# The context taps of a 31-wide depthwise convolution: three of eight channel tiles on GpSimd, as a product and a sum

## The chip, the cores and the metric

The kernel runs on one core of a Trainium2 chip. Its engines are TensorE (PE in the profile; PEld is its weight load), VectorE (DVE), ScalarE (ACT), GpSimd (POOL) and SyncE (SP), which issues all transfers here. Each engine runs its own queue in order and waits on semaphores that others raise. The metric is the device time of one execution in microseconds (us); the median of the runs is given, and lower is better.

## The reference

Two layers work on two streams of 256 tokens of 1024 channels: the context and the latent tokens. Each layer has a mixer (one input projection, a gated linear recurrence A and a convolution module B beside it, their gated sum) and a channel part (a SwiGLU in layer 0, eight experts of which each token takes two in layer 1). The second layer needs of the context only the state of the recurrence, so branch B of the context is computed in layer 0 alone. The part that the change touches:

```python
def _dwconv_seq(u, w, b, pad_l, pad_r):        # context: along the 256 tokens
    y = lax.conv_general_dilated(u, w[:, None, :], window_strides=(1,), padding=((pad_l, pad_r),),
                                 feature_group_count=u.shape[-1], ...)
    return y + b

# in _mixer, branch B
v = u_glu * jax.nn.sigmoid(g_glu)
v = _dwconv_rows(v, conv_w, conv_b) if on_grid else _dwconv_seq(v, conv_w, conv_b, CONV_PAD, CONV_PAD)
y_b = jax.nn.silu(_layernorm(v, ln_g, ln_b)) @ w_b
```

CONV_W is 31 and CONV_PAD 15. A channel of the context is thus convolved with its own 31 weights along the tokens; the latent stream is convolved along the columns of a 4 x 64 grid, so that only 7 of the 31 weights meet a token.

## The kernel before

All tiles hold 128 channels (partitions) by up to 512 columns: 256 context tokens and 256 latent ones. Eight such tiles, j = 0 to 7, make the 1024 channels.

**Matmuls.** Weights arrive as raw chunks of four pieces of 128 x 1024 float32 (`chunk`, `hold`; two raw buffers, transfers on SyncE). Each piece is split (`split`, `hilo`) into a rounded part wh on ScalarE (L156) and a remainder wl on VectorE (L157), four buffers of each, and `mm` multiplies each eighth of it three times with the activations (L283 to L285): wh with the high part nh, wh with the low part nl, wl with nh. One piece is 24 matmuls of 512 columns. A raw buffer is free for the next transfer when its four pieces are split. Between the weight chunks stand chunks of the modulation weights, with matmuls of their own (pmod, L394).

**The mixer of layer 0.** After the first projections, the loop over j makes for each tile two pieces of matmuls, pglu and pglg; then ScalarE takes tanh of pglg into v, VectorE makes v = (v + 1) * pglu (L690), and `conv_b` makes cv from v. Between them the recurrence of branch A runs (gates, scans; L555 to L592). The next loop (eight pieces) makes `gel` on ScalarE, multiplies it on VectorE by the recurrence's result (L704), and splits the product into yah on ScalarE (L156) and yal on VectorE (L157). Then follow 16 pieces for the merging gates (gab), and behind these the LayerNorm over cv (`ln_steps`), whose first step is a sum over all cv on TensorE (pcol, L294), with the branch projection beside it.

**The convolution.** `conv_b` makes cv first as the middle tap plus bias over all columns (L599), then the 30 other context taps, each one VectorE instruction over 241 to 255 columns, cv = v shifted * weight + cv (L606), then six latent taps of 64 to 192 columns (L610). All write the same cv, so that each tap waits for the one before.

**What sets the order.** The kernel is recorded in the order of its text, and a scheduler puts each engine's instructions in a fixed order by priorities and estimated times. The splits have a raised priority; `conv_b` is recorded in `later(1000)`, so its taps come 1000 places later in priority than they stand and fill the gaps between other work of VectorE. On the chip each engine keeps the fixed order, whatever happens.

**Buffers.** Tiles of the tag ya share 16 buffers: first the recurrence's results hs and the eight v, then yah and yal, later others. A yah that takes over the buffer of a v waits until the last tap of that v is done. cv has eight buffers of its own.

Of the kernel before, what the change touches and what calls it, by code (L numbers as in the profile page):

```python
# [6 lines left out]
F32 = mybir.dt.float32  # L7
# [3 lines left out]
ALU = mybir.AluOpType  # L11
AX = mybir.AxisListType

P = 128
# [3 lines left out]
TC = 256  # L18
# [21 lines left out]
WHEN0 = {4: (0, 1, -1), 5: (2,), 6: (3, -1), 7: (4,), 8: (5, -1), 9: (6,), 10: (7, -1)}  # L40
WHEN1 = {4: (-1,), 5: (2,), 6: (3,), 8: (-1,), 9: (4,), 10: (5,), 12: (-1,), 13: (6,), 14: (7,), 15: (-1,)}
LAG1 = (0, 0)
SCW = 38
RINGA, RINGB, XB = 9, 5, 1

# [88 lines left out]
class Trunk:  # L134
# [460 lines left out]
    def conv_b(self, i, j, v, cv):  # L595
        nc = self.nc
        w = lambda t: self.v(("vw", i), j * CONVW + t)
        c0 = TC if i == DEPTH - 1 else 0
        nc.vector.tensor_scalar(cv[:, c0:T], v[:, c0:T], w(15), self.v(("vb", i), j), op0=ALU.mult, op1=ALU.add)  # L599
        if c0 == 0:  # L600
            for t in range(CONVW):
                d = t - 15
                if d == 0:
                    continue
                a0, a1 = max(0, -d), TC - max(0, d)
                nc.vector.scalar_tensor_tensor(cv[:, a0:a1], v[:, a0 + d:a1 + d], w(t), cv[:, a0:a1],  # L606
                                               op0=ALU.mult, op1=ALU.add)
        for d in (-3, -2, -1, 1, 2, 3):
            a0, a1 = TC + max(0, -d) * GRID, T - max(0, d) * GRID
            nc.vector.scalar_tensor_tensor(cv[:, a0:a1], v[:, a0 + d * GRID:a1 + d * GRID], w(15 + d),  # L610
                                           cv[:, a0:a1], op0=ALU.mult, op1=ALU.add)
# [235 lines left out]
    def run(self, ctx):  # L847
# [5 lines left out]
        self.mod = [self.cst.tile([P, 48, 2], F32, tag=f"mod{i}", name=f"mod{i}") for i in range(DEPTH)]  # L853
        self.sc = self.cst.tile([P, KD, SCW], F32, tag="sc", name="sc")
        nc.gpsimd.memset(self.mod[1], 0.0)
        nc.sync.dma_start(self.sc, self.vec_d[:, NV:NV + KD * SCW].rearrange("p (k m) -> p k m", m=SCW))
        nc.sync.dma_start(xs, self.xt_d[1])
# [43 lines left out]
        def norm1(s):  # L901
            if s == 0:
                hx1.extend(self.pairs("hx"))
            self.bgs.append(self.norm_steps(1, X, s * TC, (s + 1) * TC, self.gains(1, "n1", 1), 0, hx1, LAG1[s]))

# [495 lines left out]
def layout(inputs):  # L1401
# [5 lines left out]
    xt = np.concatenate([a["ctx"][0], a["x"][0]], axis=0).T.reshape(KD, P, 2, TC).transpose(2, 1, 0, 3)  # L1407
    vec = np.zeros((P, NV + KD * SCW), f32)

    def put(key, m):  # L1410
        vec[:, VO[key]:VO[key] + m.shape[1]] = m
# [14 lines left out]
    put("fg", col(a["final_g"]))  # L1426
    cc = np.zeros((P, KD, SCW), f32)
    cc[:, :, 6] = col(a["c"][0])
# [77 lines left out]
```

## Time and profile before

| | us |
|---|---|
| median of 3 runs (1849.68 to 1850.18) | 1849.96 |
| the profiled execution | 1851.57 |
| its span, first to last instruction | 1849.5 |
| TensorE busy in it | 1805.6 |
| VectorE busy | 1220.4 |
| ScalarE busy | 815.0 |
| GpSimd busy | 0.8 |
| 240 context taps (L606) on VectorE | 102.3 |

The span is what the hardware profiler saw of one execution on the core; the execution's own time holds 2.1 us more around it. An engine's busy time is the sum of its instructions; where they overlap in the engine's pipeline, they are counted once. TensorE's granted clock is 0.991 of full speed over the whole span, and 1.00 in the stretch from 50 us on in which the mixer of layer 0 lies. That mixer spans some 60 to 460 us; the context taps lie between 119 and 301 us.

### The profile page before, as it was taken

The page shows a single profiled execution, that of the slowest core. Times are in us where ns is not written, and L with a number is a line of the kernel's source. Part 1 is how long each engine was busy: PE and PEld are TensorE (multiplying, and loading weights), DVE is VectorE, ACT ScalarE, POOL GpSimd, SP SyncE. Part 2 cuts the span into 40 slices and gives each one's busy share as a digit, 9 for nine tenths or more (in the row PEclk, how much of TensorE's full clock was granted, in tenths as well). Part 3 has the DMA queues.
Part 4 walks back from the last instruction along what each step waited for, and adds up shares of the span by engine and source line. Part 5 has one row for each costly group of instructions (what it writes and reads, how often), then busy time and mean ns, then how long its engine had stood idle before and what let it go on. Part 6 is the DMA issues. An engine that isn't in the chain of part 4 may idle for free.

```text
span 1849.5 us, 26754 instructions
## 1 busy us (share of the span) xinstructions
PE 1805.6 (98%) x10394; PEld 1380.3 (75%) x10394; DVE 1220.4 (66%) x2232; ACT 815.0 (44%) x1177; POOL 0.8 (0%) x6
## 2 busy tenths in 40 slices
PE   8999999999999999999999999999999999999996
PEld 4667777768998888889778899657865776686553
DVE  4899996255679977756899656318933972595112
ACT  3695332253552222224789564216722761474001
POOL 0000000000000000000000000000000000000000
PEclk8999999999999999999999999899999999999998
DMA  9233444231235645521233547699999999999995
GB/s 369 94 141 117 181 182 182 91 110 73 97 120 200 222 178 194 197 91 47 103 119 132 183 180 298 262 419 420 420 387 421 420 392 400 420 420 377 418 419 228
DMA packets 65654, 449.64 MB, mean 243 GB/s; under 512 B 7280, under 2 KB 7408, under 8 KB 23024
## 3 DMA queue, kind: packets, MB, share of 16 engines
q1 hardware_dynamic: 65520, 447.85, 61.6%
q8 instruction: 84, 1.38, 0.3%
q14 instruction: 50, 0.41, 0.1%
HBM read 446.78 MB, written 1.05 MB: 242 GB/s over the span
## 4 chain that ended last, share of the span: by engine, by line
PE 80%; DVE 11%; DMA 5%; ACT 2%; issue 1%; SPq 0%; ACTq 0%; DVEq 0%
PE ps L283 11%; PE ps L285 11%; PE ps L284 11%; PE s L1243 8%; DMA mraw<-in_wm_dram 4%; PE y L1298 4%; PE s L1233 3%; PE s L1232 3%; PE s L1231 3%; DVE wl L157 2%; PE y L1292 2%; PE y L1291 2%; PE y L1290 2%; PE ps L782 2%; PE ps L781 2%; PE ps L783 2%
## 5 line engine op out<-in xcount | busy, mean ns | idle before, releaser
L156 ACT ACTIVATE wh<-raw 128x1024 fp32r<-128x1024 f32 (+1 forms) x237 | 246.7, 1053 | 454.4 <-PE ps L284 287.7
L157 DVE TENSOR_TENSOR wl<-raw,wh 128x1024 fp32r<-128x1024 f32 (+1 forms) x237 | 286.4, 1216 | 132.0 <-ACT wh L156 129.1
L283 PE MATMUL ps<-nh,wh 128*128 128x512 f32 (+1 forms) x736 | 273.2, 371 | 0.7 <-ACT wh L156 0.7
L285 PE MATMUL ps<-nh,wl 128*128 128x512 f32 (+1 forms) x736 | 269.6, 367 | 3.1 <-DVE wl L157 3.1
L284 PE MATMUL ps<-nl,wh 128*128 128x512 f32 (+1 forms) x736 | 269.5, 366 | 0.0
L157 DVE TENSOR_TENSOR wl<-mraw,wh 128x1024 fp32r<-128x1024 f32 x198 | 234.0, 1222 | 24.9 <-ACT wh L156 23.8
L156 ACT ACTIVATE wh<-mraw 128x1024 fp32r<-128x1024 f32 x198 | 202.8, 1055 | 30.1 <-PE s L1232 23.6
L1243 PE MATMUL s<-mraw,xes 128*64 128x256 f32 x1760 | 205.3, 384 | 3.6 <-DMA mraw<-in_wm_dram 3.5
L1243 PEld LDWEIGHTS s<-mraw,xes 128*64 128x64 f32 x1760 | 124.6, 138 | 62.4 <-DMA mraw<-in_wm_dram 4.3
L283 PEld LDWEIGHTS ps<-nh,wh 128*128 128x128 f32 x736 | 139.1, 189 | 31.0 <-issue 2.2
L259 ACT ACTIVATE hd<-s 128x128 f32<-128x128 f32 (+1 forms) x88 | 27.9, 317 | 304.4 <-PE s L1243 279.8
L285 PEld LDWEIGHTS ps<-nh,wl 128*128 128x128 f32 x736 | 139.0, 189 | 27.9 <-DVE wl L157 3.3
L284 PEld LDWEIGHTS ps<-nl,wh 128*128 128x128 f32 x736 | 139.1, 189 | 25.5 <-issue 1.4
L1252 DVE TENSOR_TENSOR hd<-hd,s 128x128 f32<-128x128 f32 (+1 forms) x88 | 29.6, 336 | 174.1 <-ACT hd L259 174.1
L1233 PE MATMUL s<-wl,xe 128*128 128x512 f32 x264 | 104.9, 397 | 4.2 <-DVE wl L157 4.2
L1298 PE MATMUL y<-mraw,hs 128*64 128x512 f32 x440 | 104.5, 595 | 3.2 <-DMA mraw<-in_wm_dram 1.7
L1231 PE MATMUL s<-wh,xe 128*128 128x512 f32 x264 | 106.6, 404 | 0.0
L1232 PE MATMUL s<-wh,xe 128*128 128x512 f32 x264 | 103.7, 393 | 0.0
L606 DVE SCALAR_TENSOR_TENSOR cv<-v,vec,cv 128x251 f32<-128x251 f32 (+14 forms) x240 | 102.3, 469 | 0.7
L235 DVE SCALAR_TENSOR_TENSOR junk<-wv,scr 128x512 f32<-128x512 f32 x128 | 84.1, 686 | 0.2
L283 PE MATMUL pglu<-nh,wh 128*128 128x256 f32 (+1 forms) x192 | 64.6, 337 | 1.0 <-ACT wh L156 1.0
L1233 PEld LDWEIGHTS s<-wl,xe 128*128 128x128 f32 x264 | 49.5, 188 | 19.6 <-DVE wl L157 8.9
(290 smaller groups left out, 3433.8 us busy)
## 6 DMA issues: line engine op xcount, KB each, us to landing
mraw<-in_wm_dram SPq DMA_DIRECT2D x264, 1024.0 KB, 11.6
raw<-in_wd_dram SPq DMA_DIRECT2D x64, 2048.0 KB, 8.0
wv<-in_wv_dram SPq DMA_DIRECT2D x96, 256.0 KB, 3.8
lw<-in_wd_dram SPq DMA_DIRECT2D x16, 256.0 KB, 2.8
raw<-in_wd_dram SPq DMA_DIRECT2D x2, 1024.0 KB, 14.9
xs<-in_xt_dram SPq DMA_DIRECT2D x1, 1024.0 KB, 4.9
xc<-in_xt_dram SPq DMA_DIRECT2D x1, 1024.0 KB, 7.9
scr<-in_sr_dram SPq DMA_DIRECT2D x4, 256.0 KB, 8.7
```

The costliest lines, as they stand in the source:

```text
L156: return (self.nc.scalar.activation(hi, src, AF.Copy), self.nc.vector.tensor_tensor(lo, src, hi.bitcast(F32), op=ALU.subtract))
L157: self.nc.vector.tensor_tensor(lo, src, hi.bitcast(F32), op=ALU.subtract))
L235: nc.vector.scalar_tensor_tensor(junk, w[h], 1.0, rows[2 * s + h], op0=ALU.mult, op1=ALU.mult, accum_out=acc[:, h, s:s + 1])
L283: self.nc.tensor.matmul(o, wh, ah, start=(k == 0), stop=False)
L284: self.nc.tensor.matmul(o, wh, al, start=False, stop=False)
L285: self.nc.tensor.matmul(o, wl, ah, start=False, stop=(k == KD - 1))
L606: nc.vector.scalar_tensor_tensor(cv[:, a0:a1], v[:, a0 + d:a1 + d], w(t), cv[:, a0:a1], op0=ALU.mult, op1=ALU.add)
L1231: nc.tensor.matmul(p1, xe[0][:, k, :], wh[:, cs], start=(k == 0), stop=False)
L1232: nc.tensor.matmul(p1, xe[1][:, k, :], wh[:, cs], start=False, stop=False)
L1233: nc.tensor.matmul(p1, xe[0][:, k, :], wl[:, cs], start=False, stop=(k == KD - 1))
L1243: nc.tensor.matmul(p1[r, 0:2 * P].rearrange("p (g f) -> p g f", g=2), xe[:, k, :], w[:, :, h * P:(h + 1) * P], start=(k == 0), stop=(k == ...
L1298: ins = self.nc.tensor.matmul(py[0][r, :], hs[:, f * HALF:(f + 1) * HALF], raw[:, f * PIECE + q * 512:f * PIECE + (q + 1) * 512], start=(c ...
```

## The change

For the channel tiles j = 1, 3 and 5 the 30 context taps leave VectorE. Each becomes two GpSimd instructions: a product of the shifted v and the weight into a new tile tap (two buffers, in the pool of the recurrence's weights), and a sum of cv and tap into cv. The middle tap with the bias and the six latent taps of these tiles stay on VectorE. Taps of the other five tiles are as they were. In the changed program lines stand 1 (behind line 42) to 6 (behind line 606) further down: L606 is L612, L610 is L616, L156 is L157, L259 is L260.

```diff
+POOLED = (1, 3, 5)
...
                 a0, a1 = max(0, -d), TC - max(0, d)
+                if j in POOLED:
+                    p = self.lrup.tile([P, TC], F32, tag="tap", name="tap")
+                    nc.gpsimd.tensor_scalar(p[:, a0:a1], v[:, a0 + d:a1 + d], w(t), None, op0=ALU.mult)
+                    nc.gpsimd.tensor_tensor(cv[:, a0:a1], cv[:, a0:a1], p[:, a0:a1], op=ALU.add)
+                    continue
                 nc.vector.scalar_tensor_tensor(cv[:, a0:a1], v[:, a0 + d:a1 + d], w(t), cv[:, a0:a1],
                                                op0=ALU.mult, op1=ALU.add)
```

The order of TensorE and of the transfers stays. On GpSimd, behind the two memsets at the kernel's start, stood before nothing but the test at the end of the kernel (names are tiles with their buffer numbers; in brackets the semaphores that an instruction waits for):

```order
L1501 UNCONDITIONAL_BRANCH [waits barrier_Pool_Activation_PE_DVE_SP_gather]
L855 MEMSET mod1_64 128x96
L876 MEMSET wz_95 128x512
L1381 TENSOR_LOAD cint_10514 [waits DVE_49]
L1154 COMPARE_AND_BRANCH
```

Now 180 instructions and one more ahead of them stand there; tile j = 1 has v_1062 and cv_1065:

```order
L882 MEMSET wz_95 128x512
L609 ISA
L609 TENSOR_SCALAR tap_1067<-v_1062,vec_58 128x241 [waits DMAHW0_49,DVE_49]
L609 TENSOR_SCALAR tap_1070<-v_1062,vec_58 128x242
L610 TENSOR_TENSOR cv_1065<-cv_1065,tap_1067 128x241 [waits DVE_49,PE_49,Pool_49]
L610 TENSOR_TENSOR cv_1065<-cv_1065,tap_1070 128x242 [waits Pool_49]
L609 TENSOR_SCALAR tap_1073<-v_1062,vec_58 128x243
L609 TENSOR_SCALAR tap_1076<-v_1062,vec_58 128x244 [waits Pool_49]
L610 TENSOR_TENSOR cv_1065<-cv_1065,tap_1073 128x243 [waits Pool_49]
```

They come in groups of two products and two sums; three of four wait for an earlier one of GpSimd's own, and the first of a tile for VectorE.

On ScalarE, where the stage of gel begins (yah is the rounded part of gel's product, wh that of the weight pieces), the order before was:

```order
L259 ACTIVATE gel_1890<-ps_1865 128x512 [waits PE_49]
L156 ACTIVATE yah_1893<-gel_1890 128x512 [waits DVE_49]
L156 ACTIVATE wh_1982<-raw_1980 128x1024 [waits DMAHW0_49,Activation_49]
L156 ACTIVATE wh_2018<-raw_1980 128x1024 [waits Activation_49]
L156 ACTIVATE wh_2054<-raw_1980 128x1024 [waits PE_49,Activation_49]
L259 ACTIVATE gel_1926<-ps_1901 128x512 [waits PE_49]
L156 ACTIVATE yah_1929<-gel_1926 128x512 [waits DVE_49]
L156 ACTIVATE wh_2090<-raw_1980 128x1024 [waits PE_49,Activation_49]
L259 ACTIVATE gel_1973<-ps_1937 128x512 [waits PE_49]
L156 ACTIVATE yah_1976<-gel_1973 128x512 [waits DVE_49]
```

The same place now:

```order
L260 ACTIVATE gel_2070<-ps_2045 128x512 [waits PE_49]
L157 ACTIVATE yah_2073<-gel_2070 128x512 [waits DVE_49,Pool_49]
L157 ACTIVATE wh_2162<-raw_2160 128x1024 [waits DMAHW0_49,Activation_49]
L157 ACTIVATE wh_2198<-raw_2160 128x1024 [waits Activation_49]
L157 ACTIVATE wh_2234<-raw_2160 128x1024 [waits PE_49,Activation_49]
L260 ACTIVATE gel_2106<-ps_2081 128x512 [waits PE_49]
L157 ACTIVATE yah_2109<-gel_2106 128x512 [waits DVE_49,Pool_49]
L157 ACTIVATE wh_2270<-raw_2160 128x1024 [waits PE_49,Activation_49]
L260 ACTIVATE gel_2153<-ps_2117 128x512 [waits PE_49]
L157 ACTIVATE yah_2156<-gel_2153 128x512 [waits DVE_49,Pool_49]
```

The instructions are the same in the same places; the three yah, of j = 1, 2 and 3, wait for GpSimd as well.

On VectorE, just behind the v of tile j = 1 (cv_893 is the cv of tile 0, uc and gi are branch A's), the order before was:

```order
L599 TENSOR_SCALAR cv_1065<-v_1062,vec_58 128x512
L555 SCALAR_TENSOR_TENSOR gi_1110<-gi_1110,uc_709 128x512
L606 SCALAR_TENSOR_TENSOR cv_893<-v_890,vec_58,cv_893 128x250
L555 SCALAR_TENSOR_TENSOR gi_1119<-gi_1119,uc_709 128x512
L606 SCALAR_TENSOR_TENSOR cv_893<-v_890,vec_58,cv_893 128x249
L606 SCALAR_TENSOR_TENSOR cv_1065<-v_1062,vec_58,cv_1065 128x241
L606 SCALAR_TENSOR_TENSOR cv_893<-v_890,vec_58,cv_893 128x248
L157 TENSOR_TENSOR wl_1400<-raw_1397,wh_1399 128x1024
L606 SCALAR_TENSOR_TENSOR cv_893<-v_890,vec_58,cv_893 128x247
L606 SCALAR_TENSOR_TENSOR cv_1065<-v_1062,vec_58,cv_1065 128x242
```

And now:

```order
L600 TENSOR_SCALAR cv_1065<-v_1062,vec_58 128x512
L556 SCALAR_TENSOR_TENSOR gi_1170<-gi_1170,uc_709 128x512
L612 SCALAR_TENSOR_TENSOR cv_893<-v_890,vec_58,cv_893 128x250
L556 SCALAR_TENSOR_TENSOR gi_1179<-gi_1179,uc_709 128x512
L612 SCALAR_TENSOR_TENSOR cv_893<-v_890,vec_58,cv_893 128x249
L616 SCALAR_TENSOR_TENSOR cv_1065<-v_1062,vec_58,cv_1065 128x64
L612 SCALAR_TENSOR_TENSOR cv_893<-v_890,vec_58,cv_893 128x248
L158 TENSOR_TENSOR wl_1520<-raw_1517,wh_1519 128x1024
L612 SCALAR_TENSOR_TENSOR cv_893<-v_890,vec_58,cv_893 128x247
L616 SCALAR_TENSOR_TENSOR cv_1065<-v_1062,vec_58,cv_1065 128x128
```

In the places of the context taps of tile 1 stand its latent taps, which came later before.

## Rows read from the trace of the kernel before

**Rows 1.** The page, section 1: engine, busy us (share of the span), instructions.

```profile
span 1849.5 us, 26754 instructions
...
PE 1805.6 (98%) x10394; PEld 1380.3 (75%) x10394; DVE 1220.4 (66%) x2232; ACT 815.0 (44%) x1177; POOL 0.8 (0%) x6
```

**Rows 2.** Busy time by stretches of 25 us, columns in the first line.

```profile
core 0: us, PE busy (x) PEld busy (x) DVE busy (x) ACT busy (x) POOL busy (x), PEclk, DMA share, GB/s
100.00:125.00 25.00, 25.00 (x101) 18.72 (x100) 24.96 (x42) 23.62 (x33) 0.00 (x0) 1.00 0.29 106
...
175.00:200.00 25.00, 23.45 (x108) 17.34 (x107) 24.74 (x56) 5.62 (x7) 0.00 (x0) 1.00 0.69 253
200.00:225.00 25.00, 25.00 (x120) 19.13 (x119) 25.00 (x58) 7.68 (x10) 0.00 (x0) 1.00 0.44 168
...
275.00:300.00 25.00, 25.00 (x116) 18.77 (x116) 24.54 (x58) 7.31 (x10) 0.00 (x0) 1.00 0.43 169
```

**Rows 3.** Timeline of TensorE: start us, us, instruction, [idle before <- its releaser].

```profile
184.94 0.50 PE L283 MATMUL pglu<-nh,wh 128*128 128x512 f32 x1 [1.02 <-ACT wh L156]
...
186.20 0.50 PE L285 MATMUL pglu<-nh,wl 128*128 128x512 f32 x1 [0.53 <-DVE wl L157]
```

**Rows 4.** The chain of waits there, in order of time: start us, us, what.

```profile
173.72 1.13 DVE wl L157
174.87 8.94 DMA raw<-in_wd_dram
183.83 1.07 ACT wh L156
184.92 1.24 DVE wl L157
```

**Rows 5.** VectorE's last group of taps (timeline); the first use of cv (chain).

```profile
293.28 7.67 DVE L606 SCALAR_TENSOR_TENSOR cv<-v,vec,cv 128x255 f32<-128x255 f32 x15
...
359.99 1.85 PE pcol L294 x16
```

**Rows 6.** Timeline of VectorE: eight taps in a row.

```profile
203.55 3.17 DVE L606 SCALAR_TENSOR_TENSOR cv<-v,vec,cv 128x244 f32<-128x244 f32 x8
```

**Rows 7.** Busy time in four longer stretches, columns as in rows 2.

```profile
146.00:240.00 94.00, 92.45 (x419) 69.82 (x418) 93.74 (x198) 39.52 (x53) 0.00 (x0) 1.00 0.36 132
146.00:174.90 28.90, 28.90 (x121) 22.48 (x120) 28.90 (x57) 19.94 (x28) 0.00 (x0) 1.00 0.07 23
...
254.70:301.00 46.30, 46.30 (x215) 34.61 (x214) 45.75 (x103) 12.82 (x18) 0.00 (x0) 1.00 0.46 182
301.00:360.00 59.00, 59.00 (x270) 46.40 (x272) 15.50 (x15) 16.36 (x22) 0.00 (x0) 1.00 0.32 120
```

**Rows 8.** Timeline of GpSimd: its two larger instructions.

```profile
0.74 0.18 POOL L855 MEMSET mod<- 128x96 f32 x1 [0.29 <-POOLq L1495]
0.85 0.53 POOL L876 MEMSET wz<- 128x512 f32 x1
```

**Rows 9.** Timeline of ScalarE around yah of j = 1, 2, 3.

```profile
227.49 0.63 ACT L156 ACTIVATE yah<-gel 128x512 fp32r<-128x512 f32 x1 [4.44 <-DVE gel L704]
228.02 2.94 ACT L156 ACTIVATE wh<-raw 128x1024 fp32r<-128x1024 f32 x3
...
234.90 0.63 ACT L156 ACTIVATE yah<-gel 128x512 fp32r<-128x512 f32 x1 [3.46 <-DVE gel L704]
235.44 1.04 ACT L156 ACTIVATE wh<-raw 128x1024 fp32r<-128x1024 f32 x1
...
239.74 0.63 ACT L156 ACTIVATE yah<-gel 128x512 fp32r<-128x512 f32 x1 [2.77 <-DVE gel L704]
...
251.91 2.94 ACT L156 ACTIVATE wh<-raw 128x1024 fp32r<-128x1024 f32 x3
```

**Rows 10.** Timeline of VectorE: v of tiles 1, 3 and 5.

```profile
145.00 0.68 DVE L690 SCALAR_TENSOR_TENSOR v<-v,pglu 128x512 f32<-128x512 f32 x1
...
175.42 0.66 DVE L690 SCALAR_TENSOR_TENSOR v<-v,pglu 128x512 f32<-128x512 f32 x1
...
191.40 0.68 DVE L690 SCALAR_TENSOR_TENSOR v<-v,pglu 128x512 f32<-128x512 f32 x1
```

**Rows 11.** Timelines: VectorE's three splits behind these wh, and TensorE's first use.

```profile
254.74 3.49 DVE L157 TENSOR_TENSOR wl<-raw,wh 128x1024 fp32r<-128x1024 f32 x3
...
259.80 0.50 PE L283 MATMUL ps<-nh,wh 128*128 128x512 f32 x1
```

## The prediction before the run

> **What bounds the kernel now.** I read the shares of the engines first [rows 1]: TensorE is busy for 1805.6 of 1849.5 us, VectorE for 1220.4, GpSimd for 0.8. Such a share is a mean over stages, so the table of 25 us windows comes next, over the stretch in which the context taps run [rows 2]. There both engines are full: from 100 to 300 us VectorE is busy for 24.5 to 25 of every 25 us, and TensorE for 25.00 in all but one window. The timeline of TensorE shows its only two idle spells in the stretch, 1.02 and 0.53 us, at 184.94 and 186.20 us [rows 3]. The chain of waits says where they come from [rows 4]: VectorE ends a split (wl) late at 174.8, that frees a raw buffer, the next weight transfer starts at 174.87 and takes 8.94 us, then come wh, wl and the matmul. So VectorE is full, but TensorE waits for it by only 1.55 us. The rest of its work is filler: the taps, which are recorded 1000 places later than their turn and fill the gaps between the splits. The splits come in time, and the last tap, in the group that begins at 293.28, is long over when the convolution's result is summed, at 359.99 [rows 5]. Nothing waits for taps but buffers. **A VectorE with less to do can give back at most these 1.55 us** (0.08%), and a measurement of this kernel can tell about 0.2%, or 3.7 us, from no change.
>
> **What it removes.** 90 taps (three tiles of 30) of VectorE. Eight of them in a row take 3.17 us, one after the other at some 0.39 us [rows 6], so 90 × 0.39 = 35 us of VectorE. The changed order shows where these go. Between the v of tile 1 and the split that frees the raw buffer at 174.8 stand 58 instructions; by the rows' steps they make 28.7 us, against 57 in 28.90 us before [rows 7]: other taps moved up into the holes. The same holds down to the three splits at 254.74, ahead of which the changed order has its last tap. So until about 254 VectorE is as full as it was, the 35 us and some waiting fall off the end (254.7 to 301), where nothing waits for them, and even the 1.55 us stay. What the removal gives: 0.
>
> **What it adds: GpSimd's own time.** 90 products and 90 sums of 241 to 255 columns, in order, each tile's 60 starting when its v and its first term are there. No row shows such an instruction. The nearest are two memsets [rows 8]: 0.18 us for 96 columns and 0.53 us for 512, that is 0.84 ns a column and 0.10 us besides, 0.31 us for one pass over 248 columns. A product reads one tile and writes one: one pass (0.31) to two (0.52). A sum reads two: two passes (0.52) to three (0.73), and one pass (0.31) as the lowest end of all. A pair then costs 0.62 to 1.25 us; I take the middle of the ranges, (0.31 + 0.52)/2 for the product and (0.52 + 0.73)/2 for the sum, some 1.04 us, since one of the pair reads two tiles and the rows are of an instruction that reads none. In most places each waits for the one before, by the order's waits, which pushes towards the upper end. The extra first instruction that the order shows ahead of the taps (ISA) waits for nothing, so it lies 100 us before tile 1's v and costs nothing, unless it takes longer than that.
>
> **What it adds: three waits on ScalarE.** Tiles v of the taps and yah of the next stage share a ring of 16. In the changed order yah of j=1, 2 and 3 wait for GpSimd, in the built program for counts that mean: last product of tile 1, of tile 3, of tile 5. Before, these yah ran at 227.49, 234.90 and 239.74 us [rows 9]. Tile 1's v starts at 145.00, tile 3's at 175.42, tile 5's at 191.40 [rows 10], so from about 146.5 GpSimd has 81 us for 30 pairs, 88 for 60, 93 for 90. Queued behind each yah on ScalarE stand the wh of the coming weight pieces: three behind the first, one behind the second, three more (at 251.91) some way behind the third. TensorE waits for those. The cover for the third: its three splits begin on VectorE at 254.74, the first ends 1.2 us later, and TensorE takes it up at 259.80 [rows 11]; on ScalarE alone there would be some 6 us. I take 5. So **TensorE loses (the end of tile 5's products − 239.7 − 5) us**, if positive. Running alone, GpSimd would be late from (239.7 + 5 − 146.5)/90 = 1.09 us a pair.
>
> **What GpSimd does to VectorE.** This decides the sum, and no row has the two engines at work together: GpSimd is idle in all windows [rows 2]. The lower bound is no effect at all. The upper is that one of them stands still while the other works, turn by turn. Then each of the 180 GpSimd instructions waits for one VectorE instruction and the reverse. VectorE's cost is 93.74 us for 198 instructions from 146 to 240, or 0.47 each [rows 7]; GpSimd's mean is 1.04/2 = 0.52 by the middle above. But part of each is issue and wait, in which the other can go on; with the share that occupies memory at one to two passes for a product and one to two for a sum, 0.31 to 0.52, I take 0.42. The end is then at 146.5 + 180 × (0.47 + 0.42) = 307, and VectorE by then has run 180 of the 198 instructions that it had run by 240, so the splits are as late as GpSimd is: both sides agree. TensorE loses 307 − 239.7 − 5 = 62 us. It is not given back: behind 301 TensorE is again busy for 59.00 of 59.00 us [rows 7]. With 0.31 it is 146.5 + 140 = 287, a loss of 42; with 0.63 (half of 1.25), 345, a loss of 100. I take the turns rather than no effect because both engines work here on nothing but SBUF tiles, the taps, splits and sums each with two inputs.
>
> The Trainium skill states this outright. Its page "SBUF — State Buffer", section "Who interferes with whom", says that VectorE's second read port is GpSimd's only one, so that a VectorE instruction with two SBUF inputs and a GpSimd instruction that reads SBUF exclude one another: whichever starts first holds the port to its end and the other is blocked, not slowed. No run here shows it so far. By that rule the time is the one worked out for the turns, and the rival without effect falls away.
>
> **The sum.** The profiled execution took 1851.57 us (span 1849.5 and 2.1 around it), 1.6 us above the median of the runs, 1849.96. The loss is added to either: 1851.57 + 62 = 1914 for this execution, and **1849.96 + 62 = 1912 us** for the median.
>
> **Rivals.**
> 1. *Side by side, and in time.* GpSimd and VectorE don't hinder one another and a pair takes under 1.09 us; yah waits for nothing new. For it: the bounds from the memsets, 0.62 to 1.25, have their middle just below. Against it: the waits from one instruction to the next come on top. TensorE is full either way, so this ends on the other side of the forecast, not slower: 1848.4 (with the 1.55 us) to 1850. Chance 0.13.
> 2. *Side by side, but late.* No hindrance, a pair above 1.09 us. At 1.25 the end is at 146.5 + 112.5 = 259, 14 us beyond the cover: 1864. With 0.1 us (the fixed part of a memset) for each of three waits in two pairs, 1.4 a pair, 272.5 and 1878. Tile 3's last product would be at 230.5, still in time. Chance 0.20.
> 3. *VectorE always first.* GpSimd gets in only where VectorE pauses. Then yah of j=1 stands at 227.5, VectorE runs out of work behind it, and GpSimd does 90 pairs of 0.83 to 1.04 us from there, with some 15 us of VectorE between the three: 317 to 336, a loss of 72 to 91. This is the forecast's mechanism with another order; I count it there.
> 4. *Faster.* The split at 173.64 comes earlier, the transfer behind it too, and TensorE's 1.55 us vanish. It decides if a tile's taps really left that stretch; the order says no, and even so it is 1848.4, within 0.2%. For more than 3.7 us there is no idle TensorE to fill. Chance of faster by over 0.2%: 0.02.
>
> **How the numbers follow.** Turns (with 3): 0.65, at 1912, by its ends 1892 to 1950. Late alone: 0.20, 1853 to 1880. In time: 0.13. Faster: 0.02. The likeliest is the turns, so 1912. The range leaves out rivals 1 and 4 (0.15) and the top of the turns' ends, about 0.05: 1853 to 1945. Faster 0.02, same 0.13, slower 0.85.
>
> **What would show it.** In the profile of the changed kernel: VectorE's step from tap to tap from 146 us on (0.39 now; near 0.8 to 0.9 if they take turns, 0.39 if not); the spacing of the GpSimd instructions, two of them 1.8 us if turns, near 1.0 if not; ScalarE's yah <- gel waiting for GpSimd at j=2 and j=3; TensorE idle in the windows from 175 on, in sum some 60 us, for wl at first and for wh behind yah later; and the distance from 301 to the end unchanged. It is wrong if VectorE's taps keep their step beside a busy GpSimd, or if a pair takes so long by itself that the waits alone make the loss.

## The result, and the profile after

The changed kernel takes **1929.68 us** (median, 1929.44 to 1930.88), against 1849.96 for the kernel before (the median of three runs; a fourth took 2231.29 us and is not counted), some 80 us more. The measured ratio is **1.0435, with a 95% interval of 1.0423 to 1.0448**; the two medians by themselves give 1.0431. The profiled execution took 1930.88 us, its span 1929.0. The forecast was 1912, by a loss of 62.

Page of the changed kernel, busy time by engine, then the groups of the taps (busy us, mean ns | idle before); to be read against [rows 1]:

```profile
PE 1813.5 (94%) x10394; PEld 1386.0 (72%) x10394; DVE 1227.1 (64%) x2142; ACT 814.4 (42%) x1177; POOL 176.6 (9%) x186
...
L609 POOL TENSOR_SCALAR tap<-v,vec 128x241 f32<-128x241 f32 (+14 forms) x90 | 104.5, 1171 | 143.6 <-DVE v L696 143.6
L612 DVE SCALAR_TENSOR_TENSOR cv<-v,vec,cv 128x241 f32<-128x241 f32 (+13 forms) x150 | 90.0, 624 | 0.6
L610 POOL TENSOR_TENSOR cv<-cv,tap 128x241 f32<-128x241 f32 (+14 forms) x90 | 73.5, 817 | 3.5
```

VectorE has 90 instructions fewer and is busy for 6.7 us *more*. Its remaining taps take 624 ns each in the mean, 469 before. A pair on GpSimd takes 1171 + 817 ns, 1.99 us. TensorE was not busy for 1929.0 - 1813.5 = 115.5 us, against 1849.5 - 1805.6 = 43.9: 71.6 of the span's 79.5 us more are idleness. The other 7.9 are a longer busy time for the same 10394 matmuls.

The windows of the changed kernel (columns as in [rows 2]) say where:

```profile
150.00:175.00 25.00, 25.00 (x109) 20.29 (x108) 25.00 (x38) 13.23 (x18) 24.53 (x24) 1.00 0.00 1
175.00:200.00 25.00, 10.38 (x45) 6.33 (x43) 25.00 (x36) 6.57 (x8) 24.53 (x24) 0.79 0.39 137
200.00:225.00 25.00, 23.29 (x91) 18.80 (x92) 25.00 (x39) 3.67 (x4) 24.53 (x25) 0.87 0.31 116
225.00:250.00 25.00, 19.52 (x89) 14.27 (x88) 25.00 (x40) 4.01 (x5) 24.53 (x25) 0.86 0.44 161
250.00:275.00 25.00, 17.58 (x78) 12.47 (x77) 25.00 (x39) 7.13 (x10) 24.61 (x24) 0.86 0.25 92
275.00:300.00 25.00, 18.90 (x90) 13.90 (x88) 5.99 (x10) 0.00 (x0) 24.45 (x29) 0.98 0.44 160
300.00:325.00 25.00, 0.00 (x0) 0.00 (x0) 1.94 (x4) 1.11 (x2) 23.67 (x30) 0.50 0.02 9
```

There are two parts. From 150 to 275 VectorE is full, yet gets through 36 to 40 instructions in 25 us (49 to 58 before), and TensorE misses 29 us of 125. From 275 on ScalarE stands still, and from 281 on VectorE too, beside a GpSimd that works without a pause. The first loss of TensorE, in its timeline (in brackets the wait before a row and what ended it):

```profile
175.73 0.40 PE L285 MATMUL pglg<-nl,wh 128*128 128x512 f32 x1
186.71 0.79 PE L286 MATMUL pglg<-nh,wl 128*128 128x512 f32 x1 [10.58 <-DVE wl L158]
187.30 0.63 PE L284 MATMUL pglg<-nh,wh 128*128 128x512 f32 x1
```

It waits for a split: the matmul needs the wl that stands in the chain of before at 173.72 [rows 4] and begins now at 185.23 (VectorE's timeline):

```profile
185.23 1.42 DVE L158 TENSOR_TENSOR wl<-raw,wh 128x1024 fp32r<-128x1024 f32 x1
```

From 146.00 to 186.40 VectorE ran 56 instructions in 40.40 us; before, 57 took 28.90 [rows 7]. The second loss begins on ScalarE (its timeline):

```profile
262.29 0.63 ACT L157 ACTIVATE yah<-gel 128x512 fp32r<-128x512 f32 x1 [7.01 <-DVE gel L710]
...
272.24 0.63 ACT L157 ACTIVATE yah<-gel 128x512 fp32r<-128x512 f32 x1 [6.00 <-DVE gel L710]
...
322.40 0.63 ACT L157 ACTIVATE yah<-gel 128x512 fp32r<-128x512 f32 x1 [48.09 <-POOL tap L609]
...
334.55 2.93 ACT L157 ACTIVATE wh<-raw 128x1024 fp32r<-128x1024 f32 x3
```

The yah of j = 3 waits 48.09 us for the last product of tile 5; the wh behind it, at 251.91 before [rows 9], come at 334.55, and TensorE waits 41.75 us for them:

```profile
335.64 0.79 PE L284 MATMUL ps<-nh,wh 128*128 128x512 f32 x1 [41.75 <-ACT wh L157]
```

In that stretch GpSimd shows its own price (two instructions a row):

```profile
288.03 1.81 POOL L609 TENSOR_SCALAR tap<-v,vec 128x249 f32<-128x249 f32 x2
289.81 1.51 POOL L610 TENSOR_TENSOR cv<-cv,tap 128x249 f32<-128x249 f32 x2
```

A product is 0.90, a sum 0.75, a pair 1.65 us with VectorE at rest.

What hinders VectorE is seen by kind of instruction. From 150 to 240 us, the kernel before, then the changed one (split, v made from SBUF and PSUM, middle tap, a context tap, the smallest latent tap):

```profile
L157 DVE TENSOR_TENSOR wl<-raw,wh 128x1024 fp32r<-128x1024 f32 x16 | 19.0, 1218 | 0.3 <-ACT wh L156 0.3
L690 DVE SCALAR_TENSOR_TENSOR v<-v,pglu 128x512 f32<-128x512 f32 x6 | 4.1, 677 | 0.0
L606 DVE SCALAR_TENSOR_TENSOR cv<-v,vec,cv 128x250 f32<-128x250 f32 x7 | 3.3, 475 | 0.0
L610 DVE SCALAR_TENSOR_TENSOR cv<-v,vec,cv 128x64 f32<-128x64 f32 x7 | 2.0, 279 | 0.0
L599 DVE TENSOR_SCALAR cv<-v,vec 128x512 f32<-128x512 f32 x3 | 1.6, 540 | 0.0
```

```profile
L158 DVE TENSOR_TENSOR wl<-raw,wh 128x1024 fp32r<-128x1024 f32 x11 | 14.2, 1315 | 0.0
L600 DVE TENSOR_SCALAR cv<-v,vec 128x512 f32<-128x512 f32 x5 | 3.5, 708 | 0.0
L616 DVE SCALAR_TENSOR_TENSOR cv<-v,vec,cv 128x64 f32<-128x64 f32 x7 | 3.5, 500 | 0.0
L696 DVE SCALAR_TENSOR_TENSOR v<-v,pglu 128x512 f32<-128x512 f32 x5 | 3.4, 671 | 0.0
L612 DVE SCALAR_TENSOR_TENSOR cv<-v,vec,cv 128x250 f32<-128x250 f32 x4 | 2.4, 612 | 0.0
```

Only v <- v, pglu keeps its time (677 and 671): its second input lies in PSUM. The other four grow by 0.10 to 0.22 us each, the smallest the most, so not in proportion to their size: this points to a wait rather than a slower pace. The shortest, median and longest context tap from 146 to 260 us (ns, before, then after) say so too:

```profile
L606 DVE SCALAR_TENSOR_TENSOR cv<-v,vec,cv x148: 458/472/481, 145.6 to 259.3; 128x251 f32<-128x251 f32 x10, 128x250 f32<-128x250 f32 x10, 128x249 f32<-128x249 f32 x10, 128x241 f32<-128x241 f32 x10
```

```profile
L612 DVE SCALAR_TENSOR_TENSOR cv<-v,vec,cv x92: 456/676/951, 146.4 to 259.7; 128x250 f32<-128x250 f32 x7, 128x249 f32<-128x249 f32 x7, 128x248 f32<-128x248 f32 x6, 128x247 f32<-128x247 f32 x6
```

The shortest are as short as ever, the longest have about half a microsecond on top.

### The profile page after: what moved, and what is told of

It is laid out like the page before. It is cut to its first block, busy times and chain, and to the rows that moved or that the text cites. A ratio compares the mean times of both kernels' runs of the same rounds, so it can differ in the third digit from the quotient of the medians.

```text
span 1929.0 us, 26855 instructions
## 1 busy us (share of the span) xinstructions
PE 1813.5 (94%) x10394; PEld 1386.0 (72%) x10394; DVE 1227.1 (64%) x2142; ACT 814.4 (42%) x1177; POOL 176.6 (9%) x186
## 4 chain that ended last, share of the span: by engine, by line
PE 79%; POOL 9%; DVE 7%; DMA 2%; ACT 1%; issue 1%; SPq 0%; DVEq 0%; ACTq 0%
PE ps L284 10%; PE ps L286 10%; PE ps L285 10%; PE s L1249 9%; POOL tap L609 5%; PE y L1304 4%; POOL cv L610 4%; PE s L1239 3%; PE s L1238 3%; PE s L1237 3%; DMA mraw<-in_wm_dram 2%; DVE wl L158 2%; PE y L1298 2%; PE y L1297 2%; PE y L1296 2%; PE ps L788 2%
## 5 line engine op out<-in xcount | busy, mean ns | idle before, releaser
L157 ACT ACTIVATE wh<-raw 128x1024 fp32r<-128x1024 f32 (+1 forms) x237 | 246.7, 1053 | 460.3 <-PE ps L285 289.4
L157 ACT ACTIVATE wh<-mraw 128x1024 fp32r<-128x1024 f32 x198 | 202.8, 1055 | 30.1 <-PE s L1238 24.2
L260 ACT ACTIVATE hd<-s 128x128 f32<-128x128 f32 (+1 forms) x88 | 27.9, 317 | 303.5 <-PE s L1249 278.9
L609 POOL TENSOR_SCALAR tap<-v,vec 128x241 f32<-128x241 f32 (+14 forms) x90 | 104.5, 1171 | 143.6 <-DVE v L696 143.6
L612 DVE SCALAR_TENSOR_TENSOR cv<-v,vec,cv 128x241 f32<-128x241 f32 (+13 forms) x150 | 90.0, 624 | 0.6
L610 POOL TENSOR_TENSOR cv<-cv,tap 128x241 f32<-128x241 f32 (+14 forms) x90 | 73.5, 817 | 3.5
```

What stands on the lines that cost most here:

```text
L157: return (self.nc.scalar.activation(hi, src, AF.Copy), self.nc.vector.tensor_tensor(lo, src, hi.bitcast(F32), op=ALU.subtract))
L609: nc.gpsimd.tensor_scalar(p[:, a0:a1], v[:, a0 + d:a1 + d], w(t), None, op0=ALU.mult)
L610: nc.gpsimd.tensor_tensor(cv[:, a0:a1], cv[:, a0:a1], p[:, a0:a1], op=ALU.add)
```

## The experiments

**Theory:** the loss is of two parts, splits that come late while the engines hinder one another on a full VectorE, and the third yah, which waits for a GpSimd that is slow by itself. **Rivals:** the wait alone; the hindering alone; removal that gains and hides a larger loss. Differences are medians of the comparison, each kernel against the one before on the same chip (1849.1 to 1850.4).

**1. The removal alone.** In conv_b the three lines of the GpSimd taps go:

```diff
                 if j in POOLED:
-                    p = self.lrup.tile([P, TC], F32, tag="tap", name="tap")
-                    nc.gpsimd.tensor_scalar(p[:, a0:a1], v[:, a0 + d:a1 + d], w(t), None, op0=ALU.mult)
-                    nc.gpsimd.tensor_tensor(cv[:, a0:a1], cv[:, a0:a1], p[:, a0:a1], op=ALU.add)
                     continue
```

> The 30 context taps of tiles 1, 3 and 5 are left out on both engines (their sums are missing from the result); all else is as in the changed kernel. It measures the removal alone. My theory: the removal gives nothing but at most the 1.55 us in which TensorE stood idle, so 1848.4 to 1850. Rival: VectorE was a bound after all, the 35 us fewer on it let splits and transfers come earlier, and the time falls below 1846; then what GpSimd costs is larger than the 80 us measured.

Measured: 1850.17 us, ratio 1.0001 [0.9991, 1.0010]. VectorE is busy for 1185.8 us instead of 1220.4: thirty-five microseconds less on it are worth nothing, and the 80 us are the whole price of GpSimd's part.

**2. No yah waits for GpSimd.**

```diff
-        tags = {"ya": 16, "g": 16, "cv": 8, "hx": 16, "lt": 2}
+        tags = {"ya": 16, "pv": 3, "g": 16, "cv": 8, "hx": 16, "lt": 2}
...
-            v = self.t2("ya", "v")
+            v = self.t2("pv" if not last and j in POOLED else "ya", "v")
```

> The changed kernel, but the v of tiles 1, 3 and 5 get three buffers of their own, so that no yah waits for GpSimd; the 180 GpSimd instructions and their company with VectorE stay. My theory has two parts, splits that come late while the two engines hinder one another (TensorE idle some 30 to 35 us from 175 to 275 in the changed kernel) and the third yah, which waits 48 us for GpSimd and makes TensorE wait 41.7 us for wh. Without the second the time is 1880 to 1895, and TensorE's single spell of 40 us is gone. Rival 1, the wait of yah is everything and lateness before it is made up for: 1850 to 1855. Rival 2, hindering is everything and the wait only shows it: 1920 to 1930.

Measured: 1893.13 us, 1.0235 [1.0218, 1.0252], 42.8 us over before. The spell of 41.75 us is gone (TensorE's longest wait of any kind in this stretch is 7.2, for a wl), the late splits stay. Its windows:

```profile
175.00:200.00 25.00, 13.28 (x54) 8.68 (x53) 25.00 (x34) 4.38 (x5) 24.61 (x23) 0.83 0.47 167
200.00:225.00 25.00, 25.00 (x105) 19.30 (x108) 25.00 (x43) 4.92 (x6) 24.53 (x26) 0.90 0.23 86
```

Both rivals fall: it is neither 1850 nor 1930.

**3. Tile 1 alone.** `POOLED = (1,)`.

> Only tile 1's taps go to GpSimd (30 pairs); tiles 3 and 5 have theirs on VectorE, as before. GpSimd is then done near 202 us, ahead of the one yah that waits for it (227), so only hindering is left, from 145 to 202. My theory: TensorE loses what it lost there in the changed kernel, about 15 us in 175 to 200 and a little behind it, and gets none back: 1864 to 1870. Rival, only the waits of yah cost: 1850.

Measured: 1868.12 us, 1.0103 [1.0086, 1.0120], 17.8 us for 30 pairs. TensorE is busy for 13.22 us between 175 and 200 and for 22.54 between 200 and 225, full before and behind. No yah waits for GpSimd there: late splits alone.

**4. The yah's wait with a free VectorE.**

```diff
                     continue
-                nc.vector.scalar_tensor_tensor(cv[:, a0:a1], v[:, a0 + d:a1 + d], w(t), cv[:, a0:a1],
-                                               op0=ALU.mult, op1=ALU.add)
+                continue
```

> The changed kernel with the context taps of the other five tiles left out on VectorE (the result lacks them), so that VectorE has idle time from 146 on and GpSimd has its own pace more of the time. The third wait stands here on the yah of j=2, near 235 us. If GpSimd's own price (1.65 us a pair with VectorE idle) is the larger part of the loss: a pair at 1.65 to 1.9 us, tile 5's products done at 295 to 317, TensorE loses 55 to 77, time 1905 to 1927, nearly all of it in one spell, and none between 175 and 200. If the full VectorE is what makes GpSimd late: a pair near 1.1, done by 246, time below 1860.

Measured: 1909.34 us, 1.0324 [1.0307, 1.0341], 59.0 us. A window by engine, ScalarE's row, then one row of VectorE and two of TensorE:

```profile
175.00:200.00 25.00, 25.00 (x117) 18.93 (x116) 20.02 (x33) 7.08 (x9) 24.48 (x26) 1.00 0.54 213
```

```profile
310.73 0.63 ACT L157 ACTIVATE yah<-gel 128x512 fp32r<-128x512 f32 x1 [78.42 <-POOL tap L609]
```

```profile
260.34 1.17 DVE L158 TENSOR_TENSOR yal<-gel,yah 128x512 fp32r<-128x512 f32 x1 [31.15 <-POOL tap L609]
```

```profile
263.20 0.80 PE L286 MATMUL ps<-nh,wl 128*128 128x512 f32 x1 [13.04 <-DVE wl L158]
...
316.83 0.80 PE L284 MATMUL ps<-nh,wh 128*128 128x512 f32 x1 [43.62 <-ACT wh L157]
```

Nothing is lost from 175 to 200. TensorE loses in two spells, not in one as expected. With the taps gone, the ring of buffers turns differently: a yal on VectorE waits until 260.34 for the last product of tile 3, the wl behind it comes late, and TensorE waits 13.04 us. The yah of j = 2 waits until 310.73 for the last product of tile 5, and TensorE waits 43.62 us. Both are waits for a buffer that GpSimd still reads. A pair takes 1120 + 808 ns = 1.93 us: with most of VectorE's company gone, GpSimd is late by its own price.

**5. Both at once.** The edits of 2 and 4 together.

> Both at once: own buffers for the v of tiles 1, 3 and 5, so that no yah waits for GpSimd, and no context taps of the other five tiles on VectorE, so that it has idle time (the result lacks those taps). All 180 GpSimd instructions stay. If the loss is made of these two alone, late splits on a full VectorE and the wait of yah: GpSimd still needs 150 to 170 us and stretches what runs beside it, but TensorE loses nothing or next to it, 1848 to 1853. If a stretched split costs TensorE something even when VectorE has idle time: 1858 to 1880.

Measured: 1849.22 us, 0.9999 [0.9989, 1.0009], with all 180 instructions on GpSimd, at 1237 + 864 ns a pair, until some 329 us. Its splits are stretched all the same, and TensorE loses nothing (splits from 150 to 280 us, then one window):

```profile
L158 DVE TENSOR_TENSOR wl<-raw,wh 128x1024 fp32r<-128x1024 f32 x22 | 28.5, 1325 | 21.0 <-ACT wh L157 21.0
```

```profile
175.00:200.00 25.00, 25.00 (x116) 18.93 (x116) 19.66 (x31) 6.04 (x8) 24.53 (x26) 1.00 0.59 236
```

So the four corners are 1929.7 (VectorE full, yah waits), 1893.1 (full, no wait), 1909.3 (free, wait), 1849.2 (free, no wait). The parts, 43 and 59, come to more than 80 together. A TensorE that is already late meets the waiting yah later: it runs out of work for it at 293.89 in the changed kernel and at 273.21 in run 4 (335.64 - 41.75 and 316.83 - 43.62).

**6. Another place.** Tile 7 alone, its own v buffer, its GpSimd taps recorded behind the last gel with one small product of yah ahead of them:

```diff
+POOLED = (7,)
...
             ya.append((hi, lo))
+            if j == 7 and not last:
+                self.conv_b(i, 7, v, cv[7], hi)
```

> Only tile 7's 30 taps go to GpSimd, with a v buffer of its own, and behind the last yah (289 us before), where VectorE's taps are nearly over and VectorE has idle time between its splits. A pair at 1.66 us: done near 340, ahead of the sum over cv at 360. If hindering costs only where VectorE is full or where somebody waits for GpSimd: 1848 to 1852, though splits there are stretched. If each GpSimd instruction beside a split costs TensorE time wherever it lies, at the rate of the run with tile 1 alone (18 us for 30 pairs): 1860 to 1868.

Measured: 1849.01 us, 1.0000 [0.9990, 1.0010]. That yah came at 272.96 instead of 288.96, with 30 taps fewer on VectorE, so GpSimd worked from 274 on, beside a VectorE that was busy for 17.79 us from 275 to 300 (24.54 before). TensorE is busy for 25.00 us of every 25 from 200 to 375. Thirty pairs cost 18 us in one place and nothing in the other.

**7. Does writing hinder?** Memsets in place of products and sums; in the second version they stand behind tile 1's v:

```diff
+                    if t == 0:
+                        nc.gpsimd.tensor_tensor(self.wide[:, 15:TC], cv[:, 15:TC], v[:, 0:TC - 15], op=ALU.add)
+                        continue
+                    nc.gpsimd.memset(self.wide, 0.0)
+                    nc.gpsimd.memset(self.wide, 0.0)
```

> Of each pooled tile GpSimd makes one sum of v and cv, and in place of the other 58 products and sums it fills a 128x752 tile of its own with zeros (0.73 us each by the memset rows of before), so the result lacks these taps. GpSimd is then busy for some 130 us beside the same VectorE work, but it writes and does not read. If reading is what the two engines hinder one another by: VectorE's taps keep 0.39 us from one to the next, the 64-column taps 0.28 us, TensorE loses nothing, 1848 to 1852. If any GpSimd work at SBUF hinders VectorE: taps at 0.6 us and more, splits late, 1865 to 1890.

> As the run with memsets, in which nearly all of them ran ahead of tile 1's v, beside a VectorE that did few taps yet. Now the one sum of each tile writes into the tile that the memsets fill, so they stand behind it: from 146 us on, 58 for each of three tiles, 0.73 us each, to about 275, beside the taps (the result lacks the taps of tiles 1, 3 and 5). If only reading hinders: taps keep 0.47 us and 0.39 from one to the next, 1848 to 1852. If writing hinders beside taps as well: taps at 0.55 and more, 1860 to 1890.

Measured: 1848.03 (0.9992 [0.9982, 1.0002]) and 1847.80 us (0.9995 [0.9985, 1.0004]). In the first, GpSimd did nearly all its work before 146 us, so it is the second that decides. There, from 150 to 240 us (shortest/median/longest, ns):

```profile
L614 DVE SCALAR_TENSOR_TENSOR cv<-v,vec,cv x104: 452/462/477, 150.4 to 239.6; 128x247 f32<-128x247 f32 x8, 128x246 f32<-128x246 f32 x8, 128x245 f32<-128x245 f32 x8, 128x244 f32<-128x244 f32 x8
...
L600 DVE TENSOR_SCALAR cv<-v,vec x6: 529/660/995, 154.5 to 227.5; 128x512 f32<-128x512 f32 x6
...
L158 DVE TENSOR_TENSOR wl<-raw,wh x15: 1187/1208/1226, 149.3 to 234.7; 128x1024 fp32r<-128x1024 f32 x15
```

Taps and splits, which read two tiles, don't notice a GpSimd that only writes. The middle tap, which reads one, does (528 to 546 before). One of the three sums left on GpSimd shows the reverse, 5.00 us for one instruction beside taps of VectorE without a gap:

```profile
193.91 5.00 POOL L609 TENSOR_TENSOR wide<-cv,v 128x241 f32<-128x241 f32 x1
```

The Trainium skill, page "SBUF — State Buffer", section "Who interferes with whom", has both: a VectorE instruction with two SBUF inputs contends with a GpSimd instruction that reads SBUF, not with one that only writes it, and tensor_scalar, which makes the middle tap, can enter a mode on two ports in which it contends with GpSimd. The traces agree: 462 ns against 676 for taps, and a middle tap at up to 995 beside memsets. It says besides that the later one is blocked and not slowed, with which the unchanged shortest taps (456) agree.

**8. Products or sums?** With v buffers of their own as in 2: sums alone (of v, no weight), products alone, and products' place with a second input.

```diff
+                    nc.gpsimd.tensor_tensor(cv[:, a0:a1], cv[:, a0:a1], v[:, a0 + d:a1 + d], op=ALU.add)
```

```diff
                     nc.gpsimd.tensor_scalar(p[:, a0:a1], v[:, a0 + d:a1 + d], w(t), None, op0=ALU.mult)
-                    nc.gpsimd.tensor_tensor(cv[:, a0:a1], cv[:, a0:a1], p[:, a0:a1], op=ALU.add)
```

```diff
+                    nc.gpsimd.tensor_tensor(p[:, a0:a1], v[:, a0:a1], v[:, a0 + d:a1 + d], op=ALU.add)
```

> As the run with own buffers for v (no yah waits for GpSimd), but without the 90 products: each tap is one sum of cv and the shifted v, so the result lacks the weights. If hindering goes by the time that GpSimd instructions take (sum 0.75 of a pair's 1.65 us alone), this is 45% of that run's 43 us: 1865 to 1872, GpSimd done near 225. If the two-input sums alone hinder: 1885 to 1893. If the products alone do: 1850.

> As the run with own buffers for v, but without the 90 sums: the products go into tap tiles that nobody reads, so the result lacks these taps. By time: 55% of 43 us, 1870 to 1877, GpSimd done near 240 to 250. If only instructions that read two tiles hinder, the products are harmless: 1850, and VectorE's taps keep 0.39 us. If the products alone hinder: 1885 to 1893.

> As the run with products alone, but GpSimd makes tap = v + shifted v in place of v times weight: the same tiles, the same ring of two, with a second input that is read (the result lacks the taps of tiles 1, 3 and 5). Products alone cost 10 us, sums into cv 34. If it is the second input by which sums hinder VectorE more: 1878 to 1887, taps on VectorE near 0.64 us. If it is that the sums work in place on cv, one waiting for the next: 1856 to 1862, taps near 0.55 us.

Measured: sums 1883.04 (1.0183 [1.0165, 1.0201], 33.9 us), products 1859.05 (1.0051 [1.0033, 1.0069], 10.0 us), two inputs 1882.20 (1.0177 [1.0160, 1.0194], 32.8 us). The forecasts by time, 1865 to 1872 for sums and 1870 to 1877 for products, both missed, and products were not harmless (1850) either; the sums came 2 us below the 1885 to 1893 of "the sums alone". VectorE's taps from 150 to 225 us and GpSimd's group, sums, then products, then two inputs:

```profile
L610 DVE SCALAR_TENSOR_TENSOR cv<-v,vec,cv 128x250 f32<-128x250 f32 (+14 forms) x57 | 38.4, 708 | 0.0
L608 POOL TENSOR_TENSOR cv<-cv,v 128x241 f32<-128x241 f32 (+14 forms) x90 | 79.7, 885 | 172.3 <-PE pr L550 144.0 <-DVE cv L600 21.5
```

```profile
L611 DVE SCALAR_TENSOR_TENSOR cv<-v,vec,cv 128x250 f32<-128x250 f32 (+14 forms) x74 | 38.7, 555 | 0.0
L609 POOL TENSOR_SCALAR tap<-v,vec 128x241 f32<-128x241 f32 (+14 forms) x90 | 116.7, 1316 | 140.5 <-DVE v L695 140.5
```

```profile
L611 DVE SCALAR_TENSOR_TENSOR cv<-v,vec,cv 128x251 f32<-128x251 f32 (+14 forms) x54 | 38.5, 750 | 0.0
L609 POOL TENSOR_TENSOR tap<-v 128x241 f32<-128x241 f32 (+14 forms) x90 | 73.1, 849 | 161.3 <-DVE v L695 161.3
```

The two kinds share the cost differently. A product mostly waits itself (1316 ns, 900 alone) and delays a tap little; a sum mostly makes VectorE wait (885 ns, 750 alone). It is the instruction with two inputs, not the work in place on cv; whether by its second read or by being another kind of instruction (tensor_tensor for tensor_scalar) no run separates. Ten and 34 us come to about the 43 of run 2; no run shows that they must add up.

**9. Weights or constants?** In run 2's kernel:

```diff
-        nc.vector.tensor_scalar(cv[:, c0:T], v[:, c0:T], w(15), self.v(("vb", i), j), op0=ALU.mult, op1=ALU.add)
+        nc.vector.tensor_scalar(cv[:, c0:T], v[:, c0:T], 0.5, 0.25, op0=ALU.mult, op1=ALU.add)
...
-                    nc.gpsimd.tensor_scalar(p[:, a0:a1], v[:, a0 + d:a1 + d], w(t), None, op0=ALU.mult)
+                    nc.gpsimd.tensor_scalar(p[:, a0:a1], v[:, a0 + d:a1 + d], 0.5, None, op0=ALU.mult)
```

> As the run with own buffers for v, but the products of GpSimd and the middle tap of VectorE (one tile in, 128x512) take constants in place of the weights and biases of each channel (other numbers in the result, no work left out). The middle tap reads one tile and was stretched all the same (0.54 us before, 0.85 in that run). If the weights read beside the tile are why: the middle tap is at 0.54 again. If any VectorE instruction on SBUF is stretched: 0.7 to 0.9. If the weight also makes GpSimd's product dear (0.90 us with VectorE idle), it falls towards 0.75 or less and the whole gets faster than 1893 by some us; if not, it stays at 0.90.

Measured: 1897.57 us, 1.0259 [1.0242, 1.0276], 48.2 us over before and 5 more than run 2 lost: the forecast that it gets faster missed. The middle tap takes 412 ns at its shortest, with GpSimd idle, and 940 at its longest: the weights are not why it is stretched. Products take 1027 ns in the mean, 1309 in run 2, but two in a row never take less than 1.62 us (1.77 with weights), so a product's own price falls by a tenth at most. They get in sooner, GpSimd is done near 317 us (338 in run 2), and VectorE loses more: its splits take 1493 ns in the mean from 150 to 240 us, 1420 in run 2. Why products with a constant are held up less stays open.

## Why the prediction was right, and where its terms were off

- **Removal: 0.** Right, by run 1.
- **That the two engines exclude one another.** Right in kind (run 7), and not in the form of strict turns. Forecast: 0.47 + 0.42 = 0.89 us for one VectorE and one GpSimd instruction, so 58 VectorE instructions to the split that feeds TensorE's first wait would take 52 us. Measured: 56 in 40.40, 0.72 each, while GpSimd ran 38. VectorE got more than every second turn. The sign of a tap near 0.8 to 0.9 was too strong: the taps' median is 0.68 us, and some take 0.46.
- **GpSimd's price: the term that was mis-sized.** I took 1.04 us a pair, and the memsets' upper bound was 1.25; alone it is 1.65 (0.90 + 0.75), above both ends. I had a sum dearer than a product; it is the other way round. A row of an instruction that reads nothing bounds one that reads from below only. By this price alone, with no hindrance, tile 5's products end at 146.5 + 90 x 1.65 = 295, and the forecast's formula gives a loss of 295 - 239.7 - 5 = 50: rival 2 had the right mechanism for what by this estimate is more than half of the loss, at too low a price. The other 27 us up to 322.4 are what VectorE held GpSimd up by. The second of the prediction's signs of being wrong, a pair that takes so long by itself that the waits alone make the loss, thus came half true: run 4, with most of VectorE's taps gone, still loses 59.0 us.
- **The end of tile 5's products:** 307 forecast, 322.4 measured. That 307 came so near is partly luck: the price alone was 0.61 us a pair too low, the strict turns were too dear, and the two errors offset one another (1.78 us a pair forecast, (322.4 - 146.5)/90 = 1.95 measured). Put into the forecast's formula, 322.4 - 239.7 - 5 = 78; measured 80. Its form held: the wh stand as far behind the third yah as before (12.15 us, 12.17 before). But the cover was 6.8 us, not 5: TensorE goes on 75.8 us later (335.64 for 259.80) for a yah that is 82.7 us later. And from there to the end it needs 3.7 us more (1593.4 for 1589.7), a term that the sum left out; the two partly cancel. In run 4 the same formula gives 310.7 - 234.9 - 5 = 71 for 59 measured, since there the wh followed the yah sooner (5.0 us, where it was 17.0 before). The forecast put all of the loss on the third yah. In the changed kernel that wait covers the lateness of the splits, but without it 43 us stay (run 2).
- **Waits of yah at j = 2 and j = 3.** Half right. The third waits 48.09 us. The second does not: it runs at 272.24, released by VectorE's gel, since the whole stage is late by then.
- **TensorE idle from 175, for wl first and for wh later.** Right: 10.58 us for wl at 186.71, 41.75 for wh at 335.64; 71.6 us in sum, for "some 60".
- **The distance behind it.** From the third yah to the end: 1849.5 - 239.7 = 1609.8 before, 1929.0 - 322.4 = 1606.6 after. Nothing of note is given back.
- **What I left out:** behind its long idle spells TensorE is slower for a while. Behind the first, 10.58 us, matmuls begin 0.43 us apart (187.30 and behind) in place of 0.23; in the window from 300 to 325, with TensorE idle, the granted clock is 0.50, the 1.2 GHz level. TensorE's busy time is 7.9 us longer for the same matmuls. In run 2 TensorE, behind a wait of 5.11 us that ended at 199.15, is busy for all of the window from 200 to 225, yet it gets through 105 matmuls at a mean clock of 0.90; run 5 has 116 at 1.00 from 175 to 200, equally full.

## What to carry to other kernels

Work moved to GpSimd is not free because the engine stands idle. Ask three things of the place: does VectorE there run instructions with two SBUF inputs, or tensor_scalar ones, that somebody waits for; does anything take over a buffer that GpSimd still reads; and what does one instruction cost GpSimd alone, measured on one that reads as many tiles. Thirty pairs (tile 1) cost 18 us beside a full VectorE, thirty (tile 7) nothing 130 us later, and all 90 cost nothing where VectorE had slack and nobody waited; but then there was nothing to gain either, since the removal is worth 0.

## What the runs showed of the hardware that I had not expected

- On GpSimd a product of one tile with a weight (0.90 us for 249 columns) is dearer than a sum of two tiles (0.75).
- Which engine pays depends on the instruction: 90 products cost the kernel 10 us and were themselves stretched from 0.90 to 1.32; 90 sums cost 34 and were stretched from 0.75 to 0.89.
- A GpSimd that only writes leaves VectorE's two-input taps at 462 ns, and holds up its one-input middle tap to as much as 995.
- The middle tap is at 412 ns with constants and 528 with weights and biases, at its shortest, with GpSimd idle.
